# Five groups of block products in the FFN's output product, with three groups' third products at the end

## The chip, the core and the metric

The kernel runs on one core of a Trainium2 chip. The metric is the device time of one execution in microseconds (us). TensorE (PE) multiplies matrices into PSUM banks; VectorE (DVE) and ScalarE (ACT) work elementwise between SBUF and PSUM; GpSimd (POOL) does a few small operations and issues the transfers that add onto what lies in SBUF; SyncE (SP) issues the other transfers. Every engine takes its own instructions in order.

## The reference

A trunk of two layers over 256 tokens of width 1024. Each layer is a feed-forward block (FFN), a token-mixing block and a second FFN, each added to the running state `h`:

```python
for l in range(2):
    h = h + 0.5 * swiglu(rms_norm(h, ffn1_norm[l]), ffn1_w_in[l], ffn1_w_out[l])
    h = h + mixer(rms_norm(h, mix_norm[l]))           # an SSD branch and a delta-rule branch
    h = h + 0.5 * swiglu(rms_norm(h, ffn2_norm[l]), ffn2_w_in[l], ffn2_w_out[l])
return rms_norm(h, final_norm)

def swiglu(x, w_in, w_out):                            # w_in 1024 x 5632, w_out 2816 x 1024
    gate, up = jnp.split(x @ w_in, 2, axis=-1)
    return (jax.nn.silu(gate) * up) @ w_out
```

The change is in the four FFNs only; the mixer's own code is untouched.

## The kernel before

**Tiles.** The 256 tokens are two tiles of 128 (`t` = 0, 1). Weights stream from HBM as tiles of 128x1024 fp32 (512 KB). A number is held as the sum of two parts, `hi` and `lo`, and a product is three matmuls (hi·hi, hi·lo, lo·hi: `mm3` L320, `mm3w` L325). One use of a weight tile is a *take* (`take` L206). It needs a *prep* (`prep` L180): ACT copies the raw tile `wraw` to `whi`, DVE subtracts to get `wlo`. There are 5 raw buffers (NRAW) and 5 prepared ones (NSPL), so preps run up to five takes ahead of the matmuls and a load starts when the prep five raw tiles back has read its buffer. A flag `hold` lowers the lead of the preps to one during the last takes of an FFN.

**The FFN's string.** `FFN` (L37) sets the order of an FFN's work, and a planner (`plan_ffn` L106) derives from it the stream of loads and the list of preps. `f` is the first 256 of the 2816 hidden columns, computed with the tokens as rows (`tok_chunk` L334: 48 matmuls of 128x512, 4 weight tiles). Each `c` is one chunk of 128 hidden channels (`chan_chunk` L351: 48 matmuls of 128x256 into a bank `fc`, 2 weight tiles); two of them give the hidden values `g` of a pair of chunks, which are split into `gh` and `gl`. With the two chunks of `f` there are 22 chunks, numbered 0 to 21, and 11 pairs, 0 to 10; `f` is pair 0.

**The output product** multiplies the 22 chunks by `w_out` into a 2x2 grid of blocks: `po[t][n]`, token tile `t` by half `n` of the 1024 columns. Four consecutive chunks, that is two pairs (`PAIRS`), form a *group*, for which a Strassen-like scheme needs seven block products instead of eight. A product is one take with 6 matmuls of 128x512. `A` is four of the seven (banks `p5`, `p1`, `p7`, `p6`, in `block_products` L412), `B` the other three, which go into `po` (preps `q4`, `q5`, `q6`). `d` is a chunk done directly (12 matmuls). The scheme needs sums of the blocks of `g` (`block_sums` L486: four DVE subtractions and additions into `sf`, then splits into `bsa`, `bsb`, `bsc`, `bsd` by ACT and DVE) and sums of weight tiles: a group has a *kept* tile `wsum` in one of four slots `y0` to `y3`, loaded two places ahead of its `A` by SP, with a second tile added onto it by a POOL transfer (`add_to` L164); the preps of `A` add two raw tiles on DVE (`wraw<-wraw` and `wsum<-wsum,wraw`), and after the prep `q3` one more tile is added onto `wsum` by POOL. `q6` reads it at the end. A load of a kept tile stands in SP's program where the scheduler puts it: nothing ties it to its neighbours.

`join` (L421) adds the four `p` banks onto `h` through POOL transfers. `out_chunks` (L371) does the last five direct chunks for t=0 and then t=1 and lists each step's last matmul in `state["sums"]`; `residual` (L393) adds `po` onto `h` and `norm_in` (L293) computes the next block's normalised, transposed input: squares and `zz` per row (`rstd_of` L265), `hn`, eight PE transposes `hnT`, and the split into `uW`. For t=0 this chain is issued with high priority, and its place behind the PE matmul `state["sums"][5]` of the t=1 pass. `norm_vec` (L216) loads the next norm's weights `nw` behind SP's preceding load; it is called at the start of an FFN.

Of the kernel before, what the change touches and what calls it, by code (L numbers as in the profile page):

```python
# [16 lines left out]
P = 128  # L17
# [35 lines left out]
def trunk_kernel(ctx, tc, x, wst, wsm, norms, lpar, rpar, cst, out):  # L53
# [52 lines left out]
    def plan_ffn(j):  # L106


        o, j2, begun, held = j + 4 * FC, j + 4 * FC + 22, [], []
        spots, q = [], 0  # L110
        for at, kind in enumerate(FFN):
            if kind == "A":
                spots.append(at - 2)
        o1 = o + FFN[: FFN.index("A")].count("d")
        for at, kind in enumerate(FFN):
            if at in spots:
                y = len(stream)
                stream.extend([("y", o1 + 4 * q), ("+", o1 + 4 * q + 1, y)])
                begun.append(y)
                q += 1  # L120
            if kind in "fc":
                j = plan_plain(j, 4 if kind == "f" else 2)
            elif kind == "d":
                o = plan_plain(o, 1)
            elif kind == "A":
                y, u = begun.pop(0), len(stream)
                stream.extend([("w", o + 1), ("w", o + 2), ("w", o)])
                plan.append(("q1", (y, u, u + 1), u + 2))
                plan.append(("q0", (u + 2, y, u + 1), u + 3))
                plan.append(("q2", (u,), u + 3))  # L130
                plan.append(("q3", (y, o + 3), u + 3))
                held.append((y, o + 2))
                o += 4
            else:
                y, b22 = held.pop(0)
                stream.append(("w", b22))
                plan.append(("q4", (len(stream) - 1,), len(stream)))
                stream.append(("w", b22 + 1))
                plan.append(("q5", (len(stream) - 1,), len(stream)))
                plan.append(("q6", (y,), len(stream)))  # L140
        return j2

    j0 = 0
# [11 lines left out]
            m += 1  # L155
        limit.append(m)
    n_forms = len(plan)
    state = {"loaded": 0, "prepped": 0, "taken": 0, "last": None, "hold": False, "behind": {}, "late": {}, "first": 0}
    raws, halves = {}, {}

    def tile_of(i):
# [5 lines left out]
    def load(j):  # L167
        kind, i = stream[j][:2]
        if kind == "+":
            add_to(raws[stream[j][2]], i)  # L170
            return
        if kind == "y":
            r = slots.tile([P, 1024], F32, tag=f"y{state['first']}", name="wsum")
            state["first"] = (state["first"] + 1) % 4
        else:
            r = wpool.tile([P, 1024], F32, tag="wraw", name="wraw", bufs=NRAW)
        state["last"] = nc.sync.dma_start(r[:], tile_of(i))
        raws[j] = r

    def prep(i):  # L180
# [84 lines left out]
    def rstd_of(t):  # L265

        ss = small([P, 2], "ss")
        for n in range(2):
# [24 lines left out]
    def norm_in(nw, add=None):  # L293

        place_input()
        for t in range(2):
            with tc.high_priority(offset=PRI), ExitStack() as behind:
                if add:
                    added = add(t)
                    if t == 0:  # L300
                        behind.enter_context(tc.issue_after(state["sums"][5].ins))
                ins, done = rms_chain(t, nw)
            if t == 0:
                state["hold"] = False
# [85 lines left out]
                    )  # L390
                    state["sums"].append(ins)

    def residual(po, nw):  # L393
        def add(t):
            for n in range(2):
# [15 lines left out]

    def block_products(todo, begin, end):  # L412

        for bank, st, prs in todo:
            wh, wl = take()
            for i, p in enumerate(prs):
                sh, sl = st(p)
                c = slice(i * 512, (i + 1) * 512)
                mm3(bank[:], sh, sl, wh[:, c], wl[:, c], begin and i == 0, end and i == 1)

    def join(pb):  # L421

# [15 lines left out]
        onto(hv[1][1], u5)  # L438
        yield

    def close_blocks(po, stat, sums, pb, nw):

        direct, joined, n = list(DIRECT), join(pb), 0
        rest = FFN[FFN.rindex("c") + 1 :]
        for kind in rest[: len(rest) - NSPL]:
            if kind == "d":
                k = direct.pop(0)
                out_chunks(po, stat, [k], None, first=k == DIRECT[0])  # L450
                continue
# [12 lines left out]


    def ffn(nxt):
# [6 lines left out]
        bsd = s2.tile([P, 2, 2, P], F32R, tag="s2", name="bsd")  # L473
        bsb3 = bsb[:, 0:12].rearrange("p (i o j) t -> p i o j t", i=2, o=2)
        bsb1 = bsb[:, 12:16].rearrange("p (i o) t -> p i o t", i=2)

        def sums(p, j):

            q, i = (p - 1) // 2, (p - 1) % 2
# [3 lines left out]
            b = (bsc[:, 0:2], bsc[:, 2:4], bsb1, bsd[:])[q]  # L483
            return b[:, i, 0, :], b[:, i, 1, :]

        def block_sums(p, g2):  # L486
# [8 lines left out]
            q, i = (p - 1) // 2, (p - 1) % 2  # L495
# [26 lines left out]
        for c in range(FC - 1):  # L522
            g2 = tmp2("g2")
            for a in range(2):
# [721 lines left out]

    norm_in(nw0)
    for l in range(DEPTH):
        ffn(norm_vec(3 * l + 1))
        mixer(l, norm_vec(3 * l + 2))  # L1250
        add = ffn(norm_vec(3 * l + 3) if l + 1 < DEPTH else None)
    nw = norm_vec(3 * DEPTH)
    for t in range(2):
        add(t)
# [142 lines left out]
```

## Time and profile before

| what | value |
|---|---|
| median of 3 runs | 1556.36 us (1554.48 to 1556.77) |
| the profiled execution | 1555.2 us |
| its span on the core | 1553.4 us |
| PE busy | 1529.5 us (98%), 11458 matmuls |
| DVE busy | 1210.0 us (78%), 1840 instructions |
| ACT busy | 945.9 us (61%), 1534 instructions |
| HBM read | 314.50 MB, 204 GB/s over the span |

Rows of a timeline give start, duration, engine, source line, operation, output and inputs with their shapes; the brackets at the end give the time that the engine sat idle before the instruction and what ended it. `xN` counts instructions that a row joins. In groups of instructions the columns are busy time, mean ns of one, then the idle time before them with what ended it. A busy PE counts from a matmul's start to its modelled end, so that matmuls overlap; the distance from start to start is the rate. L67 is the helper of every ACT operation, L70 that of a DVE operation on two tensors, L73 that of a DVE operation with a scalar, so instructions are told apart by their tiles. L321 to L323 are the three matmuls of `mm3`, and L177 and L165 the two places at which weight loads are issued.

### The profile page before, as it was taken

Reading aid. Unit: us, or ns where it says so; the run is one execution under the profiler, and the core shown is the slowest. Engines: PE = TensorE matmul, PEld = TensorE weight load, DVE = VectorE, ACT = ScalarE, POOL = GpSimd, SP = SyncE. Lnnn points to the kernel's source line nnn. Section 1 sums busy time; section 2 is a strip of 40 time slices with the busy share of each in tenths; the row PEclk is TensorE's granted clock in tenths of the full one; section 3 lists DMA queues with packets and bytes.
Section 4 is the critical chain, followed back from the end, with each engine's and each line's share of the span. In section 5 each row is a group of like instructions: output and inputs, shape, how many; then the busy total and the mean of one; then the engine's idle time right before and its main releaser. Section 6 shows DMA issues by size and latency. Waiting matters only on the chain.

```text
span 1553.4 us, 29029 instructions
## 1 busy us (share of the span) xinstructions
PE 1529.5 (98%) x11458; PEld 1384.0 (89%) x11458; DVE 1210.0 (78%) x1840; ACT 945.9 (61%) x1534; POOL 100.7 (6%) x108
## 2 busy tenths in 40 slices
PE   8999999999999999999899999999999999999998
PEld 7999889999888888999689998899998888889996
DVE  6778768967899766878677787699579996677786
ACT  5555677765576545655455566676756665455564
POOL 0000110000000000000100011000000000000010
PEclk9999999999999999999999999999999999999999
DMA  8878775653564686678967787666446557856785
GB/s 292 262 244 261 229 224 165 190 158 109 192 202 163 212 239 200 180 241 248 313 199 209 219 258 231 206 187 187 124 126 213 178 165 223 245 179 199 226 250 156
DMA packets 103439, 322.50 MB, mean 208 GB/s; under 512 B 23350, under 2 KB 24326, under 8 KB 102279
## 3 DMA queue, kind: packets, MB, share of 16 engines
q1 hardware_dynamic: 96390, 299.68, 58.4%
q0 software_dynamic: 6912, 20.97, 8.0%
q8 instruction: 90, 1.47, 0.4%
q14 instruction: 47, 0.38, 0.1%
HBM read 314.50 MB, written 1.92 MB: 204 GB/s over the span
## 4 chain that ended last, share of the span: by engine, by line
PE 82%; DVE 6%; DMA 4%; issue 3%; ACT 3%; POOL 1%; SPq 0%; POOLq 0%; ACTq 0%; DVEq 0%
PE fc L332 9%; PE fc L326 9%; PE fc L331 9%; PE t L321 3%; PE t L322 3%; PE t L323 3%; DMA wraw<-in_wst_dram 3%; PE b L323 3%; PE b L321 3%; PE b L322 3%; PE o L323 2%; PE o L322 2%; PE o L321 2%; DVE wlo L70 2%; PE p L322 2%
## 5 line engine op out<-in xcount | busy, mean ns | idle before, releaser
L70 DVE TENSOR_TENSOR wlo<-wraw,whi 128x1024 fp32r<-128x1024 f32 x504 | 611.2, 1220 | 171.6 <-ACT whi L67 159.9
L67 ACT ACTIVATE whi<-wraw 128x1024 fp32r<-128x1024 f32 x504 | 527.7, 1058 | 275.8 <-PE fc L331 76.6
L332 PE MATMUL fc<-uW,wlo 128*128 128x256 f32 x1280 | 354.8, 277 | 0.0
L326 PE MATMUL fc<-uW,whi 128*128 128x256 f32 x1280 | 354.1, 277 | 0.0
L331 PE MATMUL fc<-uW,whi 128*128 128x256 f32 x1260 | 348.2, 276 | 0.0
L326 PEld LDWEIGHTS fc<-uW,whi 128*128 128x128 f32 x1280 | 240.3, 188 | 0.8
L332 PEld LDWEIGHTS fc<-uW,wlo 128*128 128x128 f32 x1280 | 240.5, 188 | 0.0
L331 PEld LDWEIGHTS fc<-uW,whi 128*128 128x128 f32 x1260 | 236.5, 188 | 0.8
L321 PE MATMUL t<-whi,uW 128*128 128x512 f32 x256 | 101.9, 399 | 0.0
L322 PE MATMUL t<-wlo,uW 128*128 128x512 f32 x256 | 100.9, 394 | 0.0
L323 PE MATMUL t<-whi,uW 128*128 128x512 f32 x256 | 100.6, 393 | 0.0
L321 PE MATMUL b<-whi,bh 128*128 128x512 f32 x192 | 76.2, 398 | 0.3 <-ACT bh L67 0.2
L322 PE MATMUL b<-wlo,bh 128*128 128x512 f32 x192 | 75.0, 390 | 0.0
L323 PE MATMUL b<-whi,bl 128*128 128x512 f32 x192 | 74.3, 394 | 0.3 <-DVE bl L70 0.3
L326 PE MATMUL xs<-uW,whi 128*128 128x256 f32 x256 | 72.7, 284 | 0.0
L332 PE MATMUL xs<-uW,wlo 128*128 128x256 f32 x256 | 71.3, 278 | 0.0
L331 PE MATMUL xs<-uW,whi 128*128 128x256 f32 x254 | 70.5, 277 | 0.0
L67 ACT ACTIVATE whi<-wsum 128x1024 fp32r<-128x1024 f32 x48 | 50.8, 1058 | 27.8 <-PE fc L331 23.3
L70 DVE TENSOR_TENSOR wlo<-wsum,whi 128x1024 fp32r<-128x1024 f32 x48 | 58.6, 1221 | 11.4 <-ACT whi L67 10.4
L322 PE MATMUL o<-wlo,gh 128*128 128x512 f32 x160 | 63.9, 399 | 2.5 <-DVE wlo L70 2.5
L321 PE MATMUL o<-whi,gh 128*128 128x512 f32 x160 | 63.9, 399 | 2.4 <-ACT whi L67 2.4
L165 POOL DMA_DIRECT2D wsum<-in_wst_dram x32 | 28.1, 878 | 582.3 <-DVE wlo L70 464.4
(332 smaller groups left out, 3430.4 us busy)
## 6 DMA issues: line engine op xcount, KB each, us to landing
wraw<-in_wst_dram SPq DMA_DIRECT2D x520, 512.0 KB, 5.0
wsum<-in_wst_dram POOLq DMA_DIRECT2D x32, 512.0 KB, 8.2
wsum<-in_wst_dram SPq DMA_DIRECT2D x16, 512.0 KB, 7.9
dc<-rdram SPq DMA_DIRECT2D x8, 1024.0 KB, 8.4
nw<-in_norms_dram SPq DMA_DIRECT2D x6, 512.0 KB, 6.8
h<-u POOLq DMA_DIRECT2D x12, 256.0 KB, 8.0
gb<-rdram SPq DMA_DIRECT2D x8, 256.0 KB, 5.7
h<-in_x_dram SPq DMA_DIRECT2D x4, 256.0 KB, 3.2
```

The source lines that it names most:

```text
L67: return A.activation(out=o, in_=i, func=func, **kw)
L70: return V.tensor_tensor(out=o, in0=a, in1=b, op=op)
L165: G.dma_start(out=r[:], in_=tile_of(i), accum_op=ALU.add)
L321: PE.matmul(ps, lh, rh, start=start, stop=False)
L322: PE.matmul(ps, lh, rl, start=False, stop=False)
L323: return PE.matmul(ps, ll, rh, start=False, stop=stop)
L326: PE.matmul(ps, wh, mh, start=start, stop=False)
L331: PE.matmul(ps, wh, ml, start=False, stop=False)
L332: PE.matmul(ps, wl, mh, start=False, stop=stop)
```

## The change

- **String and groups.** Four groups over pairs 1 to 8 with six direct chunks become five groups over pairs 0 to 9 with two direct chunks (20 and 21). The first four `A` each stand behind four `c`; the fifth stands behind two more `c`, right behind the chunk whose pair it uses. The two remaining `c` follow.
- **The other three products.** A letter `B` still does three products, `b` does two, and `e` is the third product of a group whose first two were done as `b`. `LATER` gives the groups' order: group 4 first, then 0, then 1, 2, 3, whose third products come last, behind the two direct chunks. The last bank to be finished is `po[1][0]`, so t=1 is added and squared in the order of halves 1, 0.
- **Kept tiles.** The fifth kept tile goes into the slot `nw` (kind `n`), so `norm_vec` is called behind the first `B` of the FFN instead of at its start. Each load of a kept tile is tied to stand behind the preceding load on SP's queue, where the planner lists it.
- **Block sums.** Pair 0 (from `f`) and pair 9 get block sums too. The transposed values of `f` are copied to SBUF (`g0`) by ACT for it. `bsd` and the new `bse` lie in the unused ends of the `g` tiles instead of a temporary buffer.
- **Transposes.** When an FFN closes, the t=0 chain of the next norm is placed behind `sums[7]` instead of `sums[5]`; the t=1 pass now has ten steps: four direct ones and six third products.

```diff
-FFN = "f" + 8 * "c" + "A" + 4 * "c" + "A" + 4 * "c" + "A" + 2 * "c" + "A" + 2 * "c" + "BdBBBddddd"
-PAIRS = [(1, 2), (3, 4), (5, 6), (7, 8)]
-DIRECT = [0, 1, 18, 19, 20, 21]
+FFN = "f" + 4 * ("cccc" + "A") + "cc" + "A" + "cc" + "BBbbbddeee"
+PAIRS = [(0, 1), (2, 3), (4, 5), (6, 7), (8, 9)]
+LATER = [4, 0, 1, 2, 3]
+DIRECT = [20, 21]
...
     def load(j):
...
+        elif kind == "n":
+            r = cpool.tile([P, D], F32, tag="nw", name="wsum")
         else:
             r = wpool.tile([P, 1024], F32, tag="wraw", name="wraw", bufs=NRAW)
-        state["last"] = nc.sync.dma_start(r[:], tile_of(i))
+        with ExitStack() as behind:
+            if kind != "w":
+                behind.enter_context(tc.issue_after(state["last"].ins))
+            state["last"] = nc.sync.dma_start(r[:], tile_of(i))
...
     def norm_in(nw, add=None):
-                        behind.enter_context(tc.issue_after(state["sums"][5].ins))
+                        behind.enter_context(tc.issue_after(state["sums"][7 if state["ffn"] else 5].ins))
...
     def close_blocks(po, stat, sums, pb, nxt):
+        for n, q in enumerate(LATER):
             todo = [
-                (po[0][1], lambda p: sums(p, 3), PAIRS[n]),
-                (po[0][0], lambda p: stat(2 * p + 1, 0), PAIRS[n]),
-                (po[1][0], lambda p: stat(2 * p + 1, 1), PAIRS[n]),
+                (po[0][1], lambda p: sums(p, 3), PAIRS[q]),
+                (po[0][0], lambda p: stat(2 * p + 1, 0), PAIRS[q]),
+                (po[1][0], third, PAIRS[q]),
             ]
-            block_products(todo, n == 0, False)
-            n += 1
-            if n % 2 == 0:
+            block_products(todo if n < n_full else todo[:2], n == 0, False)
+            if n == 0 and nxt is not None:
+                nw = norm_vec(nxt)
+            if n < 2:
                 next(joined)
         state["hold"] = True
-        out_chunks(po, stat, direct, direct[-1], group=NSPL, split=nw is None, first=False)
-        return residual(po, nw)
+        ws = [(k, take()) for k in DIRECT]
...
+        state["sums"] = []
+        for n in range(2):
+            direct(0, n)
+        state["sums"] = []
+        for n in (1, 0):
+            direct(1, n)
+        for q in LATER[n_full:]:
+            state["sums"] += block_products([(po[1][0], third, PAIRS[q])], False, q == LATER[-1])
+        return residual(po, nw, 1)
...
     def ffn(nxt):
-                    split(0, bank[:].rearrange("p (k t) -> p k t", k=2))
+                    g0 = tmp2("g2")
+                    act(g0[:], bank[:])
+                    split(0, g0[:].rearrange("p (k t) -> p k t", k=2))
+                    block_sums(0, g0)
```

**SP, around the end of layer 0's second FFN and the start of layer 1's first one.** This is SP's queue of loads in the kernel before (`wsum` is a kept tile, `wraw` a raw tile, `nw` the weights of a norm):

```order
L219 DMA nw<-in_norms_dram 128x1024
L177 DMA wraw<-in_wst_dram 128x1024 x54
L177 DMA wsum<-in_wst_dram 128x1024
L177 DMA wraw<-in_wst_dram 128x1024 x3
L177 DMA wsum<-in_wst_dram 128x1024
L177 DMA wraw<-in_wst_dram 128x1024 x2
L177 DMA wsum<-in_wst_dram 128x1024
L177 DMA wraw<-in_wst_dram 128x1024 x2
L177 DMA wsum<-in_wst_dram 128x1024
L177 DMA wraw<-in_wst_dram 128x1024 x9
L219 DMA nw<-in_norms_dram 128x1024
```

The same queue in the changed kernel, from the last kept tile of layer 0's second FFN:

```order
L182 DMA wsum<-in_wst_dram 128x1024
L182 DMA wraw<-in_wst_dram 128x1024 x20
L224 DMA nw<-in_norms_dram 128x1024
L182 DMA wraw<-in_wst_dram 128x1024 x11
L182 DMA wsum<-in_wst_dram 128x1024
L182 DMA wraw<-in_wst_dram 128x1024 x11
L182 DMA wsum<-in_wst_dram 128x1024
```

The four kept tiles of the next FFN stood among the last loads of this one; now the first of them stands eleven raw loads behind `nw`, and the next one eleven further on.

**ACT, at the last `A` of the first FFN.** In the kernel before (`sg` is the gate of the chunk just finished, `gh` the high part of its values, `whi` preps):

```order
L67 ACTIVATE whi_1705<-wraw_1558 128x1024
L67 ACTIVATE sg_1698<-fc_1640 128x256
L67 ACTIVATE whi_1717<-wraw_1572 128x1024
L67 ACTIVATE gh_173<-g2_1570 128x512
L67 ACTIVATE whi_1729<-wraw_1574 128x1024
L67 ACTIVATE whi_1741<-wraw_1581 128x1024
L67 ACTIVATE whi_1755<-wraw_1703 128x1024
```

And in the changed kernel (`bsa` are the split block sums of pair 9):

```order
L68 ACTIVATE whi_1706<-wsum_1367 128x1024
L68 ACTIVATE whi_1775<-wraw_1619 128x1024
L68 ACTIVATE sg_1759<-fc_1701 128x256
L68 ACTIVATE gh_171<-g2_1631 128x512
L68 ACTIVATE bsa_175<-sf_1764 128x384
L68 ACTIVATE gh_171<-sf_1764 128x128
L68 ACTIVATE whi_1787<-wraw_1633 128x1024
```

PE at the same place of the changed kernel, where the scheduler has cut the `A` in two:

```order
L328 MATMUL p7_583<-whi_1702,bsa_175 128x512
L326 MATMUL p6_581<-whi_1706,bsa_175 128x512
L327 MATMUL p6_581<-wlo_1707,bsa_175 128x512
L328 MATMUL p6_581<-whi_1706,bsa_175 128x512
L331 MATMUL fc_1822<-uW_108,whi_1775 128x256
L336 MATMUL fc_1822<-uW_108,whi_1775 128x256
L337 MATMUL fc_1822<-uW_108,wlo_1776 128x256
L331 MATMUL fc_1822<-uW_108,whi_1775 128x256
L333 MATMUL fc_1822<-uW_108,whi_1775 128x128
L326 MATMUL p1_582<-whi_1644,gh_171 128x512
L327 MATMUL p1_582<-wlo_1645,gh_171 128x512
L326 MATMUL p5_580<-whi_1637,bsa_175 128x512
```

The products of the group's first pair (12 matmuls) run first, then five matmuls of the next `c`, then the 12 of pair 9, which need the `gh` and `bsa` of the ACT rows above. Before, the last `A` used no value of the chunk just finished.

**DVE, at the end of the first FFN.** Before:

```order
L70 TENSOR_TENSOR wlo_2042<-wraw_1981,whi_2041 128x1024
L70 TENSOR_TENSOR wlo_2066<-wraw_2003,whi_2065 128x1024
L73 SCALAR_TENSOR_TENSOR h_78<-o_1881,h_78 128x512
L73 SCALAR_TENSOR_TENSOR h_78<-o_1882,h_78 128x512
L78 TENSOR_SCALAR zz_2136<-ss_2131 128x1
L73 SCALAR_TENSOR_TENSOR hn_2139<-h_78,zz_2136,nw_169 128x512
```

And in the changed kernel:

```order
L71 TENSOR_TENSOR wlo_2100<-wsum_786,whi_2099 128x1024
L71 TENSOR_TENSOR wlo_2154<-wsum_1119,whi_2153 128x1024
L74 SCALAR_TENSOR_TENSOR h_78<-o_1951,h_78 128x512
L74 SCALAR_TENSOR_TENSOR h_78<-o_1952,h_78 128x512
L74 SCALAR_TENSOR_TENSOR h_78<-o_1954,h_78 128x512
L79 TENSOR_SCALAR zz_2170<-ss_2165 128x1
L74 SCALAR_TENSOR_TENSOR hn_2173<-h_78,zz_2170,nw_1989 128x512
```

The last preps now read kept tiles, and the addition of t=1's first finished half stands ahead of t=0's `zz`.

More of the change, by code (lines that the diff above doesn't have):

```diff
@@ L109, in plan_ffn @@
         o, j2, begun, held = j + 4 * FC, j + 4 * FC + 22, [], []
[L110 to L114, printed above, removed]
+        later, last = list(LATER), list(LATER[FFN.count("B") :])
+        spots = [at - 2 for at, kind in enumerate(FFN) if kind == "A"]
         for at, kind in enumerate(FFN):
             if at in spots:
-                y = len(stream)
-                stream.extend([("y", o1 + 4 * q), ("+", o1 + 4 * q + 1, y)])
+                y, q = len(stream), len(begun)
+                stream.extend([("n" if q == 4 else "y", o + 4 * (q - len(held))), ("+", o + 4 * (q - len(held)) + 1, y)])
                 begun.append(y)
-                q += 1
             if kind in "fc":
@@ L134, in plan_ffn @@
             else:
[L135 to L140, printed above, removed]
+                if kind in "Bb":
+                    y, b22 = held[later.pop(0)]
+                    for i in range(2):
+                        stream.append(("w", b22 + i))
+                        plan.append((f"q{4 + i}", (len(stream) - 1,), len(stream)))
+                else:
+                    y, _ = held[last.pop(0)]
+                if kind in "Be":
+                    plan.append(("q6", (y,), len(stream)))
         return j2
@@ L157, in trunk_kernel @@
     n_forms = len(plan)
-    state = {"loaded": 0, "prepped": 0, "taken": 0, "last": None, "hold": False, "behind": {}, "late": {}, "first": 0}
+    state = {"loaded": 0, "prepped": 0, "taken": 0, "last": None, "hold": False, "behind": {}, "late": {}, "ffn": False, "halves": (0, 1), "first": 0}
     raws, halves = {}, {}
@@ L267, in rstd_of @@
         ss = small([P, 2], "ss")
-        for n in range(2):
+        for n in state["halves"]:
             junk = tmp2("junk")
@@ L391, in out_chunks, with residual @@
                     state["sums"].append(ins)
-    def residual(po, nw):
+    def residual(po, nw, first=0):
+        state["ffn"] = first == 1
         def add(t):
-            for n in range(2):
+            state["halves"] = (first, 1 - first) if t == 1 else (0, 1)
+            for n in state["halves"]:
                 hv = h[:, t, n * 512 : (n + 1) * 512]
@@ L418, in block_products @@
                 c = slice(i * 512, (i + 1) * 512)
-                mm3(bank[:], sh, sl, wh[:, c], wl[:, c], begin and i == 0, end and i == 1)
+                done.append(mm3(bank[:], sh, sl, wh[:, c], wl[:, c], begin and i == 0, end and i == 1))
+        return done
     def join(pb):
@@ L1248, in trunk_kernel @@
     for l in range(DEPTH):
-        ffn(norm_vec(3 * l + 1))
+        ffn(3 * l + 1)
         mixer(l, norm_vec(3 * l + 2))
-        add = ffn(norm_vec(3 * l + 3) if l + 1 < DEPTH else None)
+        add = ffn(3 * l + 3 if l + 1 < DEPTH else None)
     nw = norm_vec(3 * DEPTH)
```

32 lines of the change are left out of this document (19 added, 13 removed).

## The prediction

> **What bounds the kernel now.** I read the page first, for who is busy and who ends the chain.
>
> ```profile
> span 1553.4 us, 29029 instructions
> PE 1529.5 (98%) x11458; PEld 1384.0 (89%) x11458; DVE 1210.0 (78%) x1840; ACT 945.9 (61%) x1534; POOL 100.7 (6%) x108
> PE 82%; DVE 6%; DMA 4%; issue 3%; ACT 3%; POOL 1%; SPq 0%; POOLq 0%; ACTq 0%; DVEq 0%
> ```
>
> PE is the bound: it is busy for 98% of the span and carries 82% of the chain that ended last. So a change helps by fewer matmuls or by closing one of PE's few gaps, and hurts by opening one. The profiled execution took 1555.2 us, 1.8 around the span and 1.2 under the median of 1556.36. I sum against 1555.2 and add the 1.2 at the end.
>
> The price of a matmul is its distance to the next one, in PE's timeline:
>
> ```profile
> 101.32 0.39 PE L321 MATMUL p<-whi,bsb 128*128 128x512 f32 x1
> 101.55 0.39 PE L322 MATMUL p<-wlo,bsb 128*128 128x512 f32 x1
> 101.78 0.39 PE L323 MATMUL p<-whi,bsb 128*128 128x512 f32 x1
> 102.00 0.28 PE L326 MATMUL fc<-uW,whi 128*128 128x256 f32 x1
> ```
>
> Three matmuls of 128x512 take from 101.32 to 102.00: 0.227 us each, though each lasts 0.39, since they overlap.
>
> Then PE's few gaps. The largest one that the change touches is where layer 0's second FFN ends, with layer 1's first FFN right behind. SP's queue, ACT's timeline, and PE with `o` as output in two stretches (length, then busy time and count for PE, its weight loads, DVE and ACT, the granted clock, DMA share, GB/s) show it:
>
> ```profile
> 747.50 0.33 SPq L177 DMA_DIRECT2D wsum<-in_wst_dram  x1
> 751.81 0.33 SPq L177 DMA_DIRECT2D wsum<-in_wst_dram  x1
> 756.30 0.33 SPq L177 DMA_DIRECT2D wsum<-in_wst_dram  x1
> ```
>
> ```profile
> 759.98 1.06 ACT L67 ACTIVATE whi<-wraw 128x1024 fp32r<-128x1024 f32 x1 [2.53 <-DMA wraw<-in_wst_dram]
> 763.82 1.06 ACT L67 ACTIVATE whi<-wraw 128x1024 fp32r<-128x1024 f32 x1 [1.48 <-DMA wraw<-in_wst_dram]
> 767.54 1.06 ACT L67 ACTIVATE whi<-wraw 128x1024 fp32r<-128x1024 f32 x1 [2.66 <-DMA wraw<-in_wst_dram]
> ```
>
> ```profile
> 760.30:775.50 15.20, 10.44 (x27) 6.33 (x26) 0.69 (x1) 0.00 (x0) 0.78 1.05 340
> 164.00:170.00 6.00, 6.00 (x28) 4.99 (x27) 0.00 (x0) 0.00 (x0) 1.00 0.96 359
> ```
>
> Three kept tiles for the next FFN are loaded among this FFN's last raw tiles, at a DMA share of 1.05. The raw tiles come late, the preps wait for them, and PE does 27 matmuls in 15.20 us, partly at a clock of 0.78; the first FFN of layer 0 does 28 of them in 6.00 at full clock.
>
> **The change part by part.**
>
> *Fewer matmuls.* A group costs 7 x 6 = 42 matmuls, a direct chunk 12. Four groups and six direct chunks are 240, five and two 234: six fewer in each of four FFNs, 24 x 0.227 = **-5.4**. By the duration of 0.39 it would be -9.4, which double-counts the overlap.
>
> The Trainium skill's page "TensorE: Matmul & The Clock Gate", section "Back-to-back issue gap", gives about 131 ns a matmul at N=512 in a sustained stream. By it the saving would be 24 x 0.131 = -3.1; the pitch of 0.227 above does not agree with it, and I go by the trace.
>
> *The collision.* 27 matmuls at the rate of the undisturbed stretch take 27 x 6.00/28 = 5.8; the stretch lost 15.2 - 5.8 = 9.4. Tied behind its neighbour, the next FFN's first kept load stands eleven raw loads behind `nw`, in that FFN's own `c` work; no kept load is left in the tail. I take **-9.4**; the bounds are 0 (something else fills the tail) and -9.4.
>
> *The fifth group.* It stands right behind the chunk whose values it needs. The nearest rows are those of the last `A` before, whose first matmul starts at 140.40, and the durations by form:
>
> ```profile
> 140.40 0.39 PE L321 MATMUL p<-whi,bsb 128*128 128x512 f32 x1
> ```
>
> ```profile
> 141.50 0.36 ACT L67 ACTIVATE sg<-fc 128x256 f32<-128x256 f32 x1
> ```
>
> ```profile
> 143.24 0.41 DVE L70 TENSOR_TENSOR g<-sg,fc 128x256 f32<-128x256 f32 x1
> 143.57 1.22 DVE L70 TENSOR_TENSOR wlo<-wraw,whi 128x1024 fp32r<-128x1024 f32 x1
> ```
>
> ```profile
> L70 DVE TENSOR_TENSOR gl<-g,gh 128x512 fp32r<-128x512 f32 x40 | 27.3, 684 | 0.0
> L67 ACT ACTIVATE gh<-g 128x512 fp32r<-128x512 f32 x40 | 25.3, 633 | 56.5 <-DVE g L70 56.1
> L70 DVE TENSOR_TENSOR wraw<-wraw 128x1024 f32<-128x1024 f32 x16 | 19.6, 1225 | 39.0 <-DMA wraw<-in_wst_dram 39.0
> L70 DVE TENSOR_TENSOR sf<-g 128x128 f32<-128x128 f32 x64 | 18.2, 285 | 0.4
> L67 ACT ACTIVATE bsa<-sf 128x384 fp32r<-128x384 f32 x16 | 8.4, 522 | 2.9 <-DVE sf L70 2.7
> ```
>
> In the changed order PE has 12 matmuls of the first pair (12 x 0.227 = 2.72) and five of the next `c` (0.57, five times half that pitch) before it needs `gh`: from 140.40 on it is there at 143.69. The gate `sg` is queued behind one prep on ACT as before, so `g` ends at 143.24 + 0.41 = 143.65, and `gh` 0.63 later at 144.3: PE waits about 0.65. On DVE three `sf` of 0.285 end at 144.5 and `bsa` on ACT (0.52) at 145.0; by then PE has two more matmuls behind it (144.8): another 0.2. The prepared buffers that `A` holds then come free late, and with them the prep of the next `c`: I estimate 0.4 from the same chain. Together 1.27 per FFN, four times: **+5.1**. The bounds are 0, if DVE reaches `g` one prep (1.22) earlier, and +10, if it gets there one prep later (4 x 1.22 more).
>
> *The start of the first FFN.* DVE's order puts one prep ahead of the last split of the input for t=1:
>
> ```profile
> 17.39 1.22 DVE L70 TENSOR_TENSOR wlo<-wraw,whi 128x1024 fp32r<-128x1024 f32 x1
> 18.53 1.28 DVE L70 TENSOR_TENSOR uW<-hnT,uW 128x512 fp32r<-128x512 f32 x2
> ```
>
> Before, one prep already stood there; a second costs up to 1.22, most of it beside t=0's matmuls. With the norm's load gone from the start I take **+0.4**, bounds -0.4 and +1.2.
>
> *The end.* The last norm has no FFN to hide it. Behind PE's last matmul stand an addition and a product, and the new order of halves leaves one more product in front of `zz`:
>
> ```profile
> 1546.25 0.69 DVE L73 SCALAR_TENSOR_TENSOR h<-o,h 128x512 f32<-128x512 f32 x1 [1.98 <-PE o L323]
> 1546.98 0.69 DVE L70 TENSOR_TENSOR fo<-h,nw 128x512 f32<-128x512 f32 x1
> ```
>
> **+0.6**, one such row less a little idle time; bounds 0 and +0.7.
>
> *The hand-over to the next block.* The t=0 transposes stand two steps (2 x 3 x 0.227 = 1.36) further into t=1's pass, now ten steps (6.8):
>
> ```profile
> 186.83 1.03 PE L286 MATMUL hnT<-cs,hn 128*128 128x128 f32 x8
> ```
>
> ```profile
> 188.98 1.28 DVE L70 TENSOR_TENSOR uW<-hnT,uW 128x512 fp32r<-128x512 f32 x2
> ```
>
> Of the 2.15 from `hnT` to the first `uW`, DVE spent most on two preps; 1.36 later these are done, so the split can start at once and ends about when the pass does. I take 0; bounds 0 and +0.4 in each of three hand-overs. The third products' preps read kept tiles that are long in place, so no load is waited for. `join` on POOL moves one product earlier and has the whole tail for cover: 0. The pair-0 sums and the ACT copy (`g0`) stand in a stretch where ACT and DVE idle, at 0.
>
> *DVE and the loads inside the groups' stretches.* Each `cccc A` now also takes its kept load and that load's addition; before they lay at the start of the FFN, in the mixer or in the tail. Four stretches (busy time and count of PE, PEld, DVE, ACT, POOL), and the landing times over the run and where four such additions ran (30 to 60 us):
>
> ```profile
> 102.00:129.40 27.40, 27.40 (x219) 26.45 (x218) 21.69 (x33) 15.58 (x23) 0.88 (x1) 1.00 0.76 231
> 129.40:145.90 16.50, 16.50 (x123) 15.55 (x122) 15.06 (x20) 10.94 (x15) 0.87 (x1) 1.00 0.86 267
> ```
>
> ```profile
> wraw<-in_wst_dram SPq DMA_DIRECT2D x520, 512.0 KB, 5.0
> wsum<-in_wst_dram POOLq DMA_DIRECT2D x32, 512.0 KB, 8.2
> ```
>
> ```profile
> wraw<-in_wst_dram SPq DMA_DIRECT2D x9, 512.0 KB, 9.5
> wsum<-in_wst_dram POOLq DMA_DIRECT2D x4, 512.0 KB, 9.9
> ```
>
> A period of `cccc A` lasts 27.40 and moves 12 tiles (eight for `c`, three for `A`, one addition) at a DMA share of 0.76; with two more it is 0.76 x 14/12 = 0.89. The stretch with two `c` ran at 0.86 and PE lost nothing there, so most of it should stay hidden. But DVE waits, in order, for the second raw tile of its addition `wraw<-wraw`: 39.0 us before 16 of them, 2.4 each (group row above), out of 27.40 - 21.69 = 5.7 idle. So 3.3 more per period are free. I take **+2.0**, 0.5 per FFN, near the free end because 0.89 is next to the 0.86 that cost nothing; bounds 0 and +19 (first rival).
>
> *Sum:* -5.4 - 9.4 + 5.1 + 0.4 + 0.6 + 0 + 2.0 = -6.7, that is 1548.5 against the profiled 1555.2, and 1549.7 with the 1.2 to the median: **1550**.
>
> **The rivals.**
>
> *DVE's wait at the addition becomes the bound (slower).* If raw tiles land as they did between 30 and 60 us, at 9.5 instead of 5.0, the wait is 2.4 + 4.5 = 6.9, over the 5.7 by 1.2. In four periods of four FFNs that is 16 x 1.2 = 19, and without my +2.0 the time is 1549.7 - 2.0 + 19 = 1567. It begins where landing passes 5.0 + 3.3 = 8.3, and eats the whole gain at 0.54 per period, a landing of 8.8. For it speaks the `wsum` that lands in 8.2 already; against it, the same kind of stretch at 0.86. Chance 0.24.
>
> The Trainium skill's page "DMA: Bandwidth & Descriptors", section "Issuing engines are not separate DMA queues", states that transfers started by different engines run on the same 16 DMA engines and interleave. The 9.5 beside four POOL additions agrees, and by that rule SP's raw loads are slowed by the additions in each stretch, which speaks for this rival.
>
> *The tail stays late.* Another late transfer (`nw`, or the next FFN's first tiles) takes the kept loads' place: the -9.4 goes, 1549.7 + 9.4 = 1559. For it: the second FFN's end has no mixer behind it whose loads could wait. Against: 0.96 DMA share and no loss at 164 to 170. Chance 0.10.
>
> *The fifth group's wait is covered.* Then 1549.7 - 5.1 = 1545. For it: `g` need only be queued one prep earlier; against: ACT's order keeps the prep ahead of `sg`. Chance 0.12.
>
> **How the numbers follow.** The forecast has 0.54, and the rivals 0.24, 0.10 and 0.12. About 0.2% (3.1 us: 1553.2 to 1559.5) is what a measurement of this kernel can tell from no change. Faster takes the covered wait (0.12) and most of the forecast (0.48): 0.60. Same takes the late tail (0.10), the forecast's upper edge (0.06) and 0.01 of the DVE rival: 0.17. Slower is the rest of the DVE rival: 0.23. The range reaches from the covered wait with the full collision, 1542 (1545 less the two terms 2.0 and 0.6), to 1564, just under the middle of the DVE rival; the forecast's own range is 1543 to 1556.
>
> **What would show it.** Right: 24 fewer matmuls, less four where a fifth `A` lets one of the next `c` be cut in two; no `wsum` issued between the last raw loads at that hand-over, and PE doing 27 matmuls of `o` there in about 6 us at clock 1.00; PE idle for 0.8 to 0.9 us before the second half of the fifth `A`, released by `gh` and `bsa`; 20 additions `wraw<-wraw` with a mean wait below 5.7. Wrong: idle PE in front of `p` matmuls in the four regular groups, released by `wlo`, with `wraw` landing past 8.3; a DMA share near 1 in the tail again; `uW` releasing PE at a hand-over for more than 0.4.

## The result, and the profile after

The changed kernel takes 1606.12 us (median of 4 runs, 1603.43 to 1606.97), the kernel before in the same session 1555.42: a ratio of 1.0316, 95% interval 1.0297 to 1.0335. It is 50.7 us slower. The forecast was 1550, with 1542 to 1564 as its range, and a chance of 0.23 for slower.

The profiled execution took 1603.43, its span 1601.3. Its page, in the lines that answer to those shown of before:

```profile
span 1601.3 us, 29138 instructions
PE 1541.0 (96%) x11438; PEld 1383.7 (86%) x11438; DVE 1238.9 (77%) x1908; ACT 955.7 (60%) x1566; POOL 108.6 (7%) x116
PE 58%; DVE 16%; DMA 15%; issue 5%; ACT 4%; POOL 1%; SPq 1%; DVEq 0%; POOLq 0%; ACTq 0%
DMA wraw<-in_wst_dram 14%; DVE wlo L71 7%; PE fc L337 4%; PE fc L331 4%; PE fc L336 4%; PE t L326 3%; PE t L327 3%; PE t L328 3%; PE b L328 3%; PE b L327 2%; PE b L326 2%; ACT whi L68 2%; PE o L328 2%; PE o L327 1%; PE o L326 1%
```

PE carries 58% of the chain that ended last, where it carried 82%. DMA, 4% before, has 15%, nearly all of it in raw weight tiles, and DVE 16% for 6%.

I cut both spans at PE's milestones: the first `f` matmul of an FFN, its first `o` matmul (the closing products, "tail"), and the first matmul of the next block.

| part | before | after | difference | of it matmuls moved or gone |
|---|---|---|---|---|
| start to the first `f` | 9.66 | 10.12 | +0.5 | |
| four stretches `f` to `o` | 580.55 | 656.34 | +75.8 | +21.8 (24 more each) |
| four tails | 142.91 | 109.45 | -33.5 | -27.2 (30 fewer each) |
| two mixers | 812.70 | 816.69 | +4.0 | |
| behind the last matmul's start | 7.60 | 8.70 | +1.1 | |

With the matmuls at 0.227 us each, the tails gained 6.3 and the stretches ahead of them **lost 54.0**. The loss is in every FFN (10, 16, 13 and 15 us). The same cut shows it for the second FFN in the stretches of time (length, then busy time and count of PE, PEld, DVE, ACT and POOL, the clock, DMA share, GB/s), of before and of after:

```profile
596.55:741.04 144.49, 144.09 (x1123) 137.95 (x1121) 112.39 (x158) 83.30 (x115) 5.88 (x7) 1.00 0.73 226
```

```profile
609.44:775.34 165.90, 154.79 (x1147) 144.37 (x1146) 122.31 (x178) 86.60 (x124) 12.45 (x14) 0.99 0.79 237
```

PE was idle for 0.4 us of the first and for 11 of the second, at a DMA share of 0.79. What happens in one period is in the timelines of POOL, SP, DVE and PE of the first FFN, and the long DMA piece between them is from the chain that ended last:

```profile
81.60 1.78 POOL L165 DMA_DIRECT2D wsum<-in_wst_dram  x2 [28.03 <-DMA wsum<-in_wst_dram]
```

```profile
82.16 7.56 SPq L182 DMA_DIRECT2D wraw<-in_wst_dram  x5
```

```profile
87.51 10.12 DMA wraw<-in_wst_dram
```

```profile
97.73 1.23 DVE L71 TENSOR_TENSOR wraw<-wraw 128x1024 f32<-128x1024 f32 x1 [8.36 <-DMA wraw<-in_wst_dram]
98.87 0.41 DVE L71 TENSOR_TENSOR g<-sg,fc 128x256 f32<-128x256 f32 x1
99.20 1.22 DVE L71 TENSOR_TENSOR wlo<-wraw,whi 128x1024 fp32r<-128x1024 f32 x1
```

```profile
100.48 0.50 PE L337 MATMUL fc<-uW,wlo 128*128 128x256 f32 x1 [2.60 <-DVE wlo L71]
100.78 0.41 PE L331 MATMUL fc<-uW,whi 128*128 128x256 f32 x1
100.99 0.41 PE L336 MATMUL fc<-uW,whi 128*128 128x256 f32 x1
```

POOL has waited for the kept tile's load, and then starts two additions in one go: the first one onto that tile, and behind it the one that `q3` of the preceding group calls for. SP issues five raw loads beside them. The second raw tile of the next group's addition on DVE is requested at 87.51 and lands 10.1 us later; DVE stands at `wraw<-wraw` for 8.36 us, with `g` and the next prep behind it. No raw buffer comes free in that time: SP issues no load from 89.39 to 100.50, and the DMA share falls to 0.04 from 97.7 to 100.5. PE runs out of prepared tiles for 2.60 us and comes back at half rate (0.213 from start to start where 0.113 is usual). Over the run:

```profile
L71 DVE TENSOR_TENSOR wraw<-wraw 128x1024 f32<-128x1024 f32 x20 | 24.5, 1225 | 120.5 <-DMA wraw<-in_wst_dram 120.5
```

That is 6.0 each against 2.4 before, over the 5.7 us of DVE's slack in a period. The mean hides two kinds: the pair of additions is started twelve times, three times in each FFN, and the twelve waits behind a pair last 7.1 to 9.5 us (8.4 on average); the other eight, at the first and at the fifth `A`, last 1.0 to 3.8. Behind eleven of the twelve PE waits 0.8 to 3.8 us before an `fc` matmul. Before the change no two additions start less than 2.4 us apart.

### The profile page after: what moved, and what is told of

Same layout as the page of the kernel before. It is cut to its first block, busy times and chain, and to the rows that moved or that the text cites. A ratio compares the mean times of both kernels' runs of the same rounds, so it can differ in the third digit from the quotient of the medians.

```text
span 1601.3 us, 29138 instructions
## 1 busy us (share of the span) xinstructions
PE 1541.0 (96%) x11438; PEld 1383.7 (86%) x11438; DVE 1238.9 (77%) x1908; ACT 955.7 (60%) x1566; POOL 108.6 (7%) x116
## 4 chain that ended last, share of the span: by engine, by line
PE 58%; DVE 16%; DMA 15%; issue 5%; ACT 4%; POOL 1%; SPq 1%; DVEq 0%; POOLq 0%; ACTq 0%
DMA wraw<-in_wst_dram 14%; DVE wlo L71 7%; PE fc L337 4%; PE fc L331 4%; PE fc L336 4%; PE t L326 3%; PE t L327 3%; PE t L328 3%; PE b L328 3%; PE b L327 2%; PE b L326 2%; ACT whi L68 2%; PE o L328 2%; PE o L327 1%; PE o L326 1%
## 5 line engine op out<-in xcount | busy, mean ns | idle before, releaser
L337 PE MATMUL fc<-uW,wlo 128*128 128x256 f32 x1280 | 359.4, 281 | 24.0 <-DVE wlo L71 24.0
L337 PEld LDWEIGHTS fc<-uW,wlo 128*128 128x128 f32 x1280 | 242.9, 190 | 27.2 <-DVE wlo L71 26.9
L71 DVE TENSOR_TENSOR wraw<-wraw 128x1024 f32<-128x1024 f32 x20 | 24.5, 1225 | 120.5 <-DMA wraw<-in_wst_dram 120.5
L68 ACT ACTIVATE gh<-g 128x512 fp32r<-128x512 f32 x44 | 27.8, 633 | 116.1 <-DVE g L71 115.4
L71 DVE TENSOR_TENSOR wlo<-wsum,whi 128x1024 fp32r<-128x1024 f32 x60 | 72.5, 1219 | 0.2
L165 POOL DMA_DIRECT2D wsum<-in_wst_dram x40 | 35.4, 983 | 543.9 <-DMA wsum<-in_wst_dram 374.1
L68 ACT ACTIVATE whi<-wsum 128x1024 fp32r<-128x1024 f32 x60 | 62.2, 1049 | 4.1 <-PE fc L336 1.7
```

The source lines that it names most:

```text
L68: return A.activation(out=o, in_=i, func=func, **kw)
L71: return V.tensor_tensor(out=o, in0=a, in1=b, op=op)
L165: G.dma_start(out=r[:], in_=tile_of(i), accum_op=ALU.add)
L337: PE.matmul(ps, wl, mh, start=False, stop=stop)
```

## The experiments

Theory A: the transfers of a group are bunched by the tie of the kept loads; DVE waits in order. Rival B: five groups are simply more DVE and ACT work than a stretch holds. Rival C: the fifth group, without slack, and the new tail cost the time. Waits below are the mean of DVE's wait at `wraw<-wraw`.

**The tie undone, and the tie alone.** In the changed kernel's `load` the tie is taken out:

```diff
-            if kind != "w":
-                behind.enter_context(tc.issue_after(state["last"].ins))
```

> The changed kernel with one thing undone: loads of kept tiles are no longer tied behind the preceding load, so SP's order has them early again (the first FFN's in one bunch at its start, the second FFN's in the mixer). Theory A, bunched transfers: the tie puts a kept load and its POOL addition into each stretch of `c` between two `A`, beside five raw loads and the group's other POOL addition; raw tiles land 10 us after their issue, DVE stands in order at `wraw<-wraw`, PE runs dry. Without the tie the stretches ahead of the tails, which lost about 54 us over four FFNs, get nearly all of it back: about 1550 us (1545 to 1560), wait at `wraw<-wraw` 3 us or less each. Theory B, too much work on DVE and ACT in a stretch whatever the transfers do: over 1590. Theory C, the fifth group without slack and the new tail: over 1590.

Measured: 1582.48 us, ratio to before 1.0166 (1.0139 to 1.0194). Theory A had said 1550, its rivals over 1590: neither. The wait fell to 3.2, but SP's timeline shows where the scheduler put the kept loads of layer 1's first FFN:

```profile
783.74 3.33 SPq L179 DMA_DIRECT2D wsum<-in_wst_dram  x4
792.00 5.68 SPq L179 DMA_DIRECT2D wraw<-in_wst_dram  x4
```

Four at once, followed by four additions on POOL within 4 us; raw loads issued at 800 and 809 landed after 14 and 11 us, and PE stalled at 824 to 829. So the bunch was moved, not dissolved: the first FFNs of the two layers still lose 12 and 9 us. The second FFNs, which have no bunch, lose 5 and 6; in layer 0's, PE's longest waits are at the fifth `A` (1.35, 0.83 and 0.43).

The same tie, added to the kernel before:

```diff
-        state["last"] = nc.sync.dma_start(r[:], tile_of(i))
+        with ExitStack() as behind:
+            if kind != "w":
+                behind.enter_context(tc.issue_after(state["last"].ins))
+            state["last"] = nc.sync.dma_start(r[:], tile_of(i))
```

> The kernel before with the tie alone: loads of kept tiles stand behind the preceding load, four groups and everything else as before. Theory A: three to four us lost per group in 16 groups, less the 9.4 of the tail collision that goes: about 1590 us (1575 to 1600), wait at `wraw<-wraw` 5 to 7 us each. Theories B and C: about 1546, since only the collision in the tail goes.

Measured: 1568.21, ratio 1.0062 (1.0039 to 1.0086); wait 4.5. The tie alone makes the kernel slower, as only A says, but by 10 and not by 30, under the expected range: the tail of layer 0's second FFN got its 9 us back (42.85 to 33.55, with the same matmuls), and the stretches lost 18.6. The expectation counted a loss in all 16 groups; POOL's timeline has the pair in eight only, the second and third group of each FFN (a row of the first FFN):

```profile
103.25 1.77 POOL L165 DMA_DIRECT2D wsum<-in_wst_dram  x2 [30.73 <-DMA wsum<-in_wst_dram]
```

DVE's waits behind these eight are 5.9 to 8.3 us, the other eight 0.6 to 3.0. That is 2.3 us lost per pair.

**One of the two additions left out.** Both kernels are the changed one; in the first the kept tile lacks its first addition, in the second the one behind `q3`, so the closing products read wrong sums.

```diff
         if kind == "+":
-            add_to(raws[stream[j][2]], i)
             return
```

> The changed kernel without the first POOL addition onto each kept tile (20 of 40 additions; the kept tile is then not the sum that the scheme needs). The kept loads stay where the tie puts them, and no engine's elementwise work changes. Theory A: the additions are the dear part of the bunch (the page of the kernel before has 8.0% of the DMA engines' time for 20.97 MB on the POOL queue, 58.4% for 299.68 MB on the others, twice the time per MB): about 1565 us (1552 to 1580). Theories B and C: within 5 us of 1606.

```diff
-        if kind == "q3":
-            add_to(r, js[1])
```

> The changed kernel without the second POOL addition onto each kept tile (the one behind the prep q3; q6 then reads the wrong sum). Theory A: half the additions are gone as in the run without the first ones, and the two no longer start together: about 1565 us (1552 to 1580). Theories B and C: within 5 us of 1606.

Measured, one run each: 1568.79 and 1564.65. Either way 37 to 41 us come back, with DVE's and ACT's work unchanged. That rules out B. The wait is 2.8 per addition where the first is left out (55.2 us over 20) and 4.1 where the other is (82.4), and still both kernels gain 36 us in the stretches: what one addition fewer frees is not this wait alone.

**Kept loads earlier.**

```diff
-        spots = [at - 2 for at, kind in enumerate(FFN) if kind == "A"]
+        spots = [at - 4 for at, kind in enumerate(FFN) if kind == "A"]
```

Theory A2, in this expectation and the next two, is theory A with a second part: some 20 us lost at the fifth `A`, whose preps come late.

> The changed kernel with each kept tile's load four places ahead of its `A` instead of two, still tied behind the preceding load. The load's first POOL addition then runs in the middle of a stretch of `c` and no longer together with the group's other one and with the raw loads of the next `A`. Theory A2: most of the 34 us of the regular groups come back and the fifth group's 20 stay: about 1575 (1568 to 1585). If the amount of transfers per stretch decides, not when they run: within 5 us of 1606.

Measured: 1565.91 (8 runs), ratio 1.0045 (1.003 to 1.0061), 2 us under the expected range. All transfers and all elementwise work are those of the changed kernel; only the time of the kept loads differs, and 40 us come back. Its groups by form and a stretch of POOL's timeline:

```profile
L71 DVE TENSOR_TENSOR wraw<-wraw 128x1024 f32<-128x1024 f32 x20 | 24.5, 1225 | 48.5 <-DMA wraw<-in_wst_dram 48.5
```

```profile
67.21 0.88 POOL L165 DMA_DIRECT2D wsum<-in_wst_dram  x1 [17.32 <-DMA wsum<-in_wst_dram]
77.55 0.88 POOL L165 DMA_DIRECT2D wsum<-in_wst_dram  x1 [9.47 <-DVE wlo L71]
95.99 0.88 POOL L165 DMA_DIRECT2D wsum<-in_wst_dram  x1 [17.57 <-DMA wsum<-in_wst_dram]
105.46 0.88 POOL L165 DMA_DIRECT2D wsum<-in_wst_dram  x1 [8.59 <-DVE wlo L71]
```

The additions of these rows start nine us apart or more (7.2 at the least in the whole run), and the wait is 2.4, as before the change. It is the bunching, not the amount.

**The fifth `A` behind all `c`,** with the loads as they were, and with the earlier loads:

```diff
-FFN = "f" + 4 * ("cccc" + "A") + "cc" + "A" + "cc" + "BBbbbddeee"
+FFN = "f" + 5 * ("cccc" + "A") + "BBbbbddeee"
```

> The changed kernel with the fifth `A` two `c` later, behind all of them (string f, five times cccc A, then BBbbbddeee); its kept tile moves two `c` later with it. Theory A2 (two parts: about 34 us from bunched transfers in the four regular groups of each FFN, about 20 from the fifth `A`, which stands only two `c` behind the fourth and whose preps come late by 5 us in each FFN): 1606 less 20, about 1586 (1580 to 1592). Theory A (transfers alone, the fifth group only its 0.6 wait for `gh`): about 1602. Theory C (the fifth group alone): about 1550.

> Both: the fifth `A` behind all `c`, and each kept load four places ahead of its `A`. Theory A2: both losses gone; what is left is fewer matmuls (-5.4), the tail without its collision (-9.4), and some 7 us at the hand-overs, in the mixers and at the end: about 1550 (1546 to 1560), a little faster than before. Theories A and C: 1570 or more, since one of the two losses would stay.

Measured: 1643.83 and 1589.05, ratios 1.0554 (1.0529 to 1.0579) and 1.0199 (1.0182 to 1.0216); they were expected 58 and 39 us lower, a miss. In the second the stretches did what was expected: with early loads they took 603.5, only 1.2 over 580.55 + 21.8. In the first they did not: 659.9, where 20 less than 656.3 was expected. With the loads as they were, the fifth group there gets its pair of additions like the others (16 pairs; DVE's waits behind them are 7.1 to 9.5 us). At the 3.4 us that a pair costs in the changed kernel (41 over 12, below), four more cost 14, about what the two `c` more gain (12, below). And the tails grew, by 40 us in the first and 30 in the second. ACT's and PE's timelines of the second (profiled at 1579.6, its fastest run) show why:

```profile
170.94 1.06 ACT L68 ACTIVATE whi<-wsum 128x1024 fp32r<-128x1024 f32 x1 [6.82 <-DMA wsum<-in_wst_dram]
```

```profile
172.04 0.79 PE L326 MATMUL o<-whi,gh 128*128 128x512 f32 x1 [5.98 <-ACT whi L68]
```

The addition behind the fifth group's `q3` takes 9 us (issued at 161.79 by POOL), and the closing products begin with that very group: `LATER` starts with 4. The two `c` behind the fifth `A` had hidden it. Over the run ACT waits 24.5 us for it:

```profile
L68 ACT ACTIVATE whi<-wsum 128x1024 fp32r<-128x1024 f32 x60 | 62.5, 1054 | 40.4 <-DMA wsum<-in_wst_dram 24.5 <-PE fc L336 15.2 <-PE fc L337 0.6
```

**Group 4 closed second, and third,** both with the fifth `A` behind all `c` and early loads:

```diff
-LATER = [4, 0, 1, 2, 3]
+LATER = [0, 4, 1, 2, 3]
-            if n == 0 and nxt is not None:
+            if n == 1 and nxt is not None:
```

> As the run with the fifth `A` last and early kept loads, but the closing products begin with group 0 and take group 4 second (`LATER` 0, 4, 1, 2, 3; the norm's weights are loaded one product later). Theory: the 30 us that that run loses in its tails come from the POOL addition behind the fifth group's prep `q3`: it takes 8 to 9 us to land, `q6` of group 4 reads the sum, and group 4 is closed right behind its `A`. Three takes more (18 matmuls, 4.1 us) in between take some 4 us, and the slow clock behind the wait, from each tail: about 1568 us (1560 to 1576). If another transfer (the norm's weights, the next block's tiles) makes the tail late: within 5 us of 1589.

```diff
-FFN = "f" + 5 * ("cccc" + "A") + "BBbbbddeee"
-LATER = [4, 0, 1, 2, 3]
+FFN = "f" + 5 * ("cccc" + "A") + "BBBbbddee"
+LATER = [0, 1, 4, 2, 3]
-                        behind.enter_context(tc.issue_after(state["sums"][7 if state["ffn"] else 5].ins))
+                        behind.enter_context(tc.issue_after(state["sums"][5].ins))
-            if n == 0 and nxt is not None:
+            if n == 2 and nxt is not None:
```

> As above with group 4 third (`LATER` 0, 1, 4, 2, 3; string f, five times cccc A, BBBbbddee, so that two third products instead of three are kept for the end; transposes behind index 5 of eight steps). Same theory: 36 matmuls, 8.2 us, in between, as long as the addition takes: the tails are free of it and the whole is about 1550 us (1546 to 1558). If another transfer makes the tail late: over 1575.

Measured: 1575.04 and 1553.21, ratios 1.0117 (1.0089 to 1.0146) and 0.9974 (0.9957 to 0.999): steps of 14 and 22 us between the medians, both inside their ranges. With group 4 second, ACT still waits 8.1 us for kept tiles; with group 4 third, no prep of ACT waits for a kept tile's transfer any more:

```profile
L68 ACT ACTIVATE whi<-wsum 128x1024 fp32r<-128x1024 f32 x60 | 62.8, 1053 | 9.7 <-PE fc L336 8.4 <-PE fc L337 0.6 <-ACT whi L68 0.6
```

That the late addition makes the tails late is shown by these waits; that it is the whole of the second step is not, since the 8.1 us are less than the 22 and the string and the place of the transposes changed as well. Five groups are then 0.26% faster than the kernel before (0.1 to 0.43%). Of the 14.8 that the matmuls (5.4) and the collision (9.4) should give, most goes in the tails (7 us over their matmuls and transposes), the mixers (3.5), the stretches (2.0) and the end (1.1).

**The transposes.**

```diff
-                        behind.enter_context(tc.issue_after(state["sums"][7 if state["ffn"] else 5].ins))
+                        behind.enter_context(tc.issue_after(state["sums"][5].ins))
```

> The changed kernel with t=0's transposes of an FFN's end behind the fifth index of the steps again instead of the seventh. If these two steps cost what the trace of the changed kernel shows at the hand-overs (PE waits 0.5 for `uW` and 1.0, before 0.5, for t=1's `hn`, in each of three): 3 us less, about 1603. If the order of the halves and of DVE's additions makes these waits and not the place of the transposes: within 1 us of 1606.

Measured, one run: 1611.73. Neither: undoing this step made the three tails with a hand-over 1.7 us longer each (29.7 on average for 27.9), where PE waits 1.1 for `hn`. So, by these tails, the two steps gain 5 us in the changed kernel; they are not a cost.

**The kernel before with the tie (its diff stands above) and early kept loads,** so four groups, no other part of the change:

```diff
-                spots.append(at - 2)
+                spots.append(at - 4)
```

> The kernel before (four groups) with the tie and each kept load four places ahead of its `A`. The tie alone measured 1568, of which 18 us are lost in the stretches of `c`; moved ahead, the kept load's addition no longer runs with the group's other one. Theory of the bunched transfers: these 18 go and the tail stays free of its collision: about 1549 us (1546 to 1554). If only the number of transfers in a stretch counts: within 4 us of 1568.

Measured: 1547.71 (5 runs), ratio 0.995 (0.9932 to 0.9968), the fastest of all. Its profile:

```profile
span 1548.7 us, 29035 instructions
PE 1527.3 (99%) x11458; PEld 1382.6 (89%) x11458; DVE 1208.1 (78%) x1840; ACT 942.0 (61%) x1534; POOL 101.2 (7%) x108
```

The stretches take 580.6, as before, and the tail of layer 0's second FFN 33.7 for 42.85. No two additions start less than 9 us apart.

So the whole gain over the kernel before comes from the tie and the early loads. With the loads dealt with alike, four groups (1547.71) beat five with group 4 third (1553.21, the same session) by 5.5 us. In the two profiles, 3.6 us apart, five groups save 5.4 in matmuls and lose 2.0 in the stretches, 4.5 in the tails, 1.8 in the mixers and 1.1 at the end. No run shows a gain from the fifth group itself.

## Why the prediction was wrong, step by step

- **DVE and the loads inside the groups' stretches (forecast +2.0, bounds 0 and +19): this step failed.** Moving the kept loads out of their bunch gives back 40.7 of the 54.0 us of the stretches (656.3 to 615.7), so this term is about **+41**, where the forecast had +2.0. (Taken in the other order, the fifth `A` first, the stretches went from 656.3 to 659.9 and then, with early loads, to 603.5: the fifth `A` alone gives nothing back while its own load makes a pair.) Its direction was the first rival's, which I gave 0.24; three things were mis-sized.

  First, I counted an addition as one tile of transfer. The page of before has the price: `q0` (POOL's queue) 8.0% of the DMA engines' time for 20.97 MB, `q1` 58.4% for 299.68 MB; 0.38% and 0.19% per MB. An addition is two tiles' worth, and the period's share goes from 0.76 to 0.76 x 16/13 = 0.94, not 0.89.

  Secondly, I took the mean share of a period for the measure. The periods of the first FFN had means of only 0.76 to 0.84; what counted was that two additions and five raw loads start within 8 us and that DVE waits in order for one of them.

  Thirdly, I priced the overrun of DVE's slack as the only loss. Twelve waits of 8.4 overrun the 5.7 by 2.7 each, 32 of the 41. A period of 27.4 became about 31: while DVE stands, no buffer comes free, so that the transfers pause behind it, and three of PE's eleven longer waits, that of 2.60 among them, are followed by matmuls at half rate (about 5 us in all four stretches). The stretch at a share of 0.86, which I held against the rival, had one addition in it, not two at once.

  The sign of being wrong came, but not where I had put it: PE's idle time stood before `fc` matmuls, not `p`, and over the run a raw tile still landed after 5.2 us in the median; of the 336 loads whose landing the trace tells, 40 took over 8.3.
- **Fifth group (+5.1, bounds 0 and +10): the term too small.** (Its three parts add to 1.25, not 1.27, which changes it by 0.1.) The wait for `gh` came as predicted: forecast 0.65, measured 0.59 beyond the usual pitch in each of the four FFNs (0.43 by the trace's own count):

```profile
156.88 0.50 PE L327 MATMUL p<-wlo,bsa 128*128 128x512 f32 x1 [0.83 <-DVE wlo L71]
159.01 0.50 PE L326 MATMUL p<-whi,gh 128*128 128x512 f32 x1 [0.43 <-ACT gh L68]
```

  The larger part stands ahead of it: the preps of the fifth `A` come late, since only two `c` lie between it and the fourth (the 0.83 of the first row, 0.7 to 0.8 in all four FFNs, and 1.4 and 1.2 more in the two second ones). Together it is 12.2 us (615.7 to 603.5 when this `A`, and its load with it, moves behind all `c`, early loads in both), just over my upper end.
- **The collision (-9.4): right.** The tail of layer 0's second FFN went from 42.85 to 27.76; 6.8 of that are its 30 matmuls, so 8.3 were gained, with the hand-over's cost in it. The tie alone gave 9.3.
- **Fewer matmuls (-5.4): right** in number (11438: 24 fewer, and four that are cut in two); the pitch did not change.
- **Start (+0.4):** 0.5, but this shows little: in the other profiles of five groups the same part takes 9.2 to 10.6. **End (+0.6): 1.1,** too small; `zz` starts 1.94 us behind the last addition (rows below, of after) and 1.48 before (1546.25 above and the last row), so the added product cost 0.46; the other 0.6 lies behind the last DVE operation, in the storing of the output, which I had not looked at. What makes it longer is open: the two kernels with an addition left out have the same order and take 7.6 and 7.7 for the whole part, as before the change:

```profile
1593.03 0.69 DVE L74 SCALAR_TENSOR_TENSOR h<-o,h 128x512 f32<-128x512 f32 x1 [1.23 <-PE o L328]
1593.75 1.29 DVE L71 TENSOR_TENSOR fo<-h,nw 128x512 f32<-128x512 f32 x2
1594.97 0.21 DVE L79 TENSOR_SCALAR zz<-ss 128x1 f32<-128x1 f32 x1
```

```profile
1547.73 0.21 DVE L78 TENSOR_SCALAR zz<-ss 128x1 f32<-128x1 f32 x1
```

- **Hand-over (0, bounds 0 and +0.4 each): too small.** In the blocks that follow, PE waits 0.5 for `uW` and 1.0, before 0.5, for t=1's `hn` (0.36 and 0.83, before 0.38, by the trace's own count). The three tails with a hand-over also keep some 1 us each over their matmuls and transposes, in waits for `wlo` preps 9 to 12 us ahead of their ends, and the mixers are 2.4 and 1.6 longer. What of the mixers' 4 us belongs to the hand-over was not separated; with four groups and the tie, without any change at the hand-over, the two mixers together are 2.6 (late loads) and 1.6 (early ones) longer.

What remains open: the five-group version with group 4 third still loses 7 us in three of its four tails, with single preps that come 0.7 to 1.0 us late; no run was made to remove them. Why a pair costs 3.4 us in the changed kernel (41 over 12) and 2.3 in the kernel before with the tie is open.

## What to carry to other kernels

Before moving a transfer "to where there is room", lay out what else starts within its landing time, on every queue, and which in-order engine stands waiting for the slowest of them: a mean DMA share of 0.8 hides a bunch that stops the loop. Price a transfer that adds onto memory from the queue's own share per MB, not as one more copy. And where a product is closed right behind the group that prepares it, count the transfer in between; the work that seems to stand in the way may be its cover.

## What the runs showed of the hardware that was not expected

- A transfer that adds onto SBUF takes about twice the DMA engines' time per MB of a plain load (0.38% against 0.19% of the span, from the page of before, where the few transfers of `join`, additions too, are on the same queue). Whether this is the addition or POOL's queue is open: POOL issues no plain load of weights in any run.
- After 2.60 us of idle time PE's next 16 matmuls ran at 0.213 us instead of 0.113, and the granted clock of the stretch was 0.61 (first row below, from 99.80 to 104.20, of the changed kernel). The length of the idle time alone does not decide it: in the same run the matmuls behind 2.76 us (the rows from 893.98 on) kept 0.11 to 0.12. Of the eleven such waits in this run only those of 2.60, 3.53 and 3.78 were followed by the slow rate; with the fifth `A` behind all `c` and late loads, one of 1.81 (at 679.01) was and one of 3.57 (at 162.46) was not. What decides it was not tested. The rows:

```profile
99.80:104.20 4.40, 3.72 (x18) 3.73 (x19) 4.40 (x6) 0.94 (x2) 0.00 (x0) 0.61 0.50 151
104.20:107.30 3.10, 3.10 (x30) 3.10 (x29) 3.03 (x7) 2.42 (x5) 0.00 (x0) 1.00 0.71 271
```

```profile
893.98 0.38 PE L337 MATMUL fc<-uW,wlo 128*128 128x256 f32 x1 [2.76 <-DVE wlo L71]
894.21 0.28 PE L331 MATMUL fc<-uW,whi 128*128 128x256 f32 x1
894.32 0.29 PE L336 MATMUL fc<-uW,whi 128*128 128x256 f32 x1
894.44 0.28 PE L337 MATMUL fc<-uW,wlo 128*128 128x256 f32 x1
```
